# A two-block transformer kernel: modulation sums, probability scaling, post-norm rows and skip columns moved to other places

## The chip, the cores and the metric

The kernel runs on one core of a Trainium2 chip. The metric is device time in microseconds, the median of three runs. The core has a matrix engine (TensorE, PE in the profile, with its weight loads as PEld), VectorE (DVE), ScalarE (ACT), GpSimd (POOL) and a DMA-issuing engine (SyncE, SP). Each engine works through its own line of instructions in order and waits on semaphores where it needs another engine's result or a transfer.

## The reference, cut to what matters

512 tokens of width 1024 pass through a first block and a second block of two layers. In all of them a conditioning vector c gives shifts, scales and gates through a 1024 x 6144 matrix per block or layer (the modulation).

```python
# first block
mod = silu(c) @ w_ada + b_ada                       # six vectors of 1024
h = rms_norm(x, norm_mix) * (1 + sc_m) + sh_m
y = fox_mixer(h, ...)                               # 16 heads of 64, causal, logits + F[t] - F[s]
x = x + g_m * y
h = rms_norm(x, norm_mlp) * (1 + sc_f) + sh_f
x = x + g_f * (square(relu(h @ w_mlp_in)) @ w_mlp_out)
# second block, layer 0: state space (ssd) + latent attention; layer 1: gated linear attention + sparse attention
for layer in range(2):
    shift_m, scale_m, gate_m, shift_f, scale_f, gate_f = silu(c) @ w + b
    h = rmsnorm(x, pre_m) * (1 + scale_m) + shift_m
    x = x + gate_m * rmsnorm(mixers[layer](h), post_m)      # post row = gate * post gain
    h = rmsnorm(x, pre_f) * (1 + scale_f) + shift_f
    x = x + gate_f * rmsnorm((silu(h @ w_gate) * (h @ w_up)) @ w_down, post_f)
# in the ssd mixer: y = ssd(...) + d_skip[:, None] * xs     # one skip factor per head of 64
```

All of it is in float32. The kernel splits each float32 operand into a high and a low part (hi, lo) and does three products (hi hi, hi lo, lo hi).

## The kernel before, in words

The class `Kernel` builds the program stage by stage; a planner of the language (the tile framework) puts each engine's instructions in an order, from their order in the program (a priority), dependencies and its own costs, and gives each tile a buffer of a pool. `self.order(later, earlier)` fixes an order by hand. `behind(n)` lowers the priority of what is inside by n.

*Weights* (`unit`, L130 to 165): each 512 KB piece is loaded on SP (L140), cast to hi on ScalarE (L151), and its lo part subtracted on DVE (L152). `mm3` issues the three products (L120 to L122).

*Start* (`first_modulation`, `first_norm`): x is loaded, then for c = 0, 1 (halves of the width) and part 1, 0 (scale, shift) a piece of the modulation: eight blocks k of 128 rows of w_ada, each multiplied by a column of silu(c) and added up, on DVE (L915, L917) or, for the k in `PADA`, by PE into PSUM (L912). PE then sums the DVE accumulator over partitions with ones (L919); DVE adds the bias (L922) and, for the scale, makes gs. `first_norm` squares x (L385), normalises it (L942), and transposes it with PE (L947) into tiles that ScalarE copies (L949), in two halves, one after each piece of c = 0. `scaled(c)` makes h_hi (L892) and, through a scaled copy that overwrites xt (L894 on ScalarE for odd k, L896 on DVE for even k), h_lo (L897).

*Attention of the first block* (`fox`): eight pairs of heads. `fox_prep` projects q, k, v of a pair; `rsqrt_many` makes the roots on DVE (L750 to L758) and L667 scales q and k by them; `fox_pair` transposes (L733) and splits them, and copies the key's high part to the other half of the partitions on GpSimd (L742). `fox_attend` does four query blocks per head, of 128, 256, 384 and 512 keys: logits on PE (L686 to L688), bias and minimum on DVE (L470), exponential on ScalarE (L99), reciprocal on DVE (L480), scaling of the probabilities (L488 on ScalarE or L490 on DVE by `share`, which is 0 here), transposes (L500) and products with v (L537 to L540). A `Feed` mixes the next pair's preparation into these steps and runs the background modulation (`bg`, `modulation_piece`) for three more of the six vectors. With `ada_tile` set, as here, DVE does its first product (L263), ScalarE the other seven in place (L265), and GpSimd adds them (L266).

*Modulation later on*: in the MLP and FFN stages `bg` accumulates on DVE (L263, L268). With `ada_lag` set, `modulation_pair` folds the accumulator's halves of partitions on GpSimd (a copy L287 and an addition L288) and PE sums two pieces at once (L294).

*State space mixer* (`ssd`, phase mixB2): an own small tile d_col is loaded by two GpSimd transfers (L1255), DVE makes eight diagonal matrices of it (L1258), and PE adds the skip with them (L1354).

*Output projections* (`down_blocks`): per pair of token blocks, per half c of the width and per block, PE makes 128 x 512; `evict` (here `add_to`) adds it to y (L1457) and squares the sum (L385). After c = 1, `post` makes the root of the block (`token_rsqrt`, L391 to L398), then per half u = y * root * row (L1379), x += u (L1380) and, if another norm follows, the squares of x. `normalized` (L436) and `modulate` (transposes L417, scalings L421 to L428) make the next h from it. At the very end `store_x` (L461) writes x.

## Time and profile before

| what | value |
|---|---|
| median of 3 runs | 2299.11 us (2297.29 to 2301.78) |
| the profiled execution | 2299.34 us, its span 2297.5 us |
| mean granted TensorE clock | 0.98 |
| PE, DVE, ACT, POOL busy | 96%, 64%, 47%, 12% of the span |
| moved by DMA | 274.82 MB, mean 120 GB/s |
| chain that ended last | PE 71%, DVE 14%, ACT 6%, DMA 5%, issue 3% |

The profile shows one execution. A row of a group gives line, engine, operation, output <- inputs and shape, a count, busy us and the mean ns of one, and then the idle time ahead of it with its releaser. A row of waits gives the waiting engine and line, what released it, the total us, the number of waits and the longest. A row of the timeline gives start, length, the instruction, and in brackets the idle time ahead of it. A row of the DMA issues gives destination <- source, queue, count, KB of one, and us from issue to landing (a median). PE's busy time is modelled from pipelined matmuls.

### The profile page before, as it was taken

The page shows a single profiled execution, that of the slowest core. Times are in us where ns is not written, and L with a number is a line of the kernel's source. Part 1 is how long each engine was busy: PE and PEld are TensorE (multiplying, and loading weights), DVE is VectorE, ACT ScalarE, POOL GpSimd, SP SyncE. Part 2 cuts the span into 40 slices and gives each one's busy share as a digit, 9 for nine tenths or more (in the row PEclk, how much of TensorE's full clock was granted, in tenths as well). Part 3 has the DMA queues.
Part 4 walks back from the last instruction along what each step waited for, and adds up shares of the span by engine and source line. Part 5 has one row for each costly group of instructions (what it writes and reads, how often), then busy time and mean ns, then how long its engine had stood idle before and what let it go on. Part 6 is the DMA issues. An engine that isn't in the chain of part 4 may idle for free.

```text
span 2297.5 us, 31560 instructions
## 1 busy us (share of the span) xinstructions
PE 2196.5 (96%) x11520; PEld 1845.2 (80%) x11520; DVE 1473.4 (64%) x3232; ACT 1081.9 (47%) x2132; POOL 266.8 (12%) x298
## 2 busy tenths in 40 slices
PE   6899999999999999899999999999999999999998
PEld 6778778788878777778988888877888878888886
DVE  5888877665537898586655563754899557322425
ACT  5677655333234656456432132644777346332322
POOL 0333200110000100210001010101434000000000
PEclk8999999999999999999999999999999999999999
DMA  7544245654533222214556463243111343331412
GB/s 228 149 147 147 65 133 179 229 198 147 176 121 117 75 66 65 37 41 153 165 177 199 160 206 101 85 121 109 31 49 32 98 142 92 110 110 56 138 47 82
DMA packets 210523, 274.82 MB, mean 120 GB/s; under 512 B 19488, under 2 KB 134896, under 8 KB 209600
## 3 DMA queue, kind: packets, MB, share of 16 engines
q1 hardware_dynamic: 205424, 254.03, 35.5%
q0 software_dynamic: 3648, 14.44, 2.3%
q10 hardware_dynamic: 1296, 4.34, 0.5%
q8 instruction: 91, 1.49, 0.3%
q14 instruction: 64, 0.52, 0.1%
HBM read 264.31 MB, written 8.45 MB: 119 GB/s over the span
## 4 chain that ended last, share of the span: by engine, by line
PE 71%; DVE 14%; ACT 6%; DMA 5%; issue 3%; SPq 0%; POOL 0%; DVEq 0%; ACTq 0%; POOLq 0%
PE mm L120 21%; PE mm L122 21%; PE mm L121 21%; DVE wlo L152 1%; ACT whi L151 1%; DVE p L490 1%; DMA ada<-w_ada 1%; DVE pt L116 1%; PE tp L500 1%; DVE p L470 1%; DMA hid<-w_ada 1%; PE o L1618 1%; PE tot L417 1%; PE yd L1310 1%; DMA d_col<-l_d_skip 1%
## 5 line engine op out<-in xcount | busy, mean ns | idle before, releaser
L120 PE MATMUL mm<-h_hi,whi 128*128 128x512 f32 (+1 forms) x920 | 330.9, 360 | 0.8 <-ACT hid L1014 0.4
L121 PE MATMUL mm<-h_lo,whi 128*128 128x512 f32 (+1 forms) x920 | 329.4, 358 | 0.1
L122 PE MATMUL mm<-h_hi,wlo 128*128 128x512 f32 (+1 forms) x920 | 329.1, 358 | 0.4 <-DVE wlo L152 0.4
L152 DVE TENSOR_TENSOR wlo<-wraw,whi 128x1024 fp32r<-128x1024 f32 (+3 forms) x194 | 235.9, 1220 | 135.9 <-ACT whi L151 134.7
L151 ACT CAST whi<-wraw 128x1024 fp32r<-128x1024 f32 (+3 forms) x194 | 199.5, 1032 | 195.5 <-PE mm L121 88.0
L120 PE MATMUL mm<-whi,h_hi 128*128 128x256 f32 (+3 forms) x544 | 192.0, 356 | 7.0 <-ACT whi L151 4.5
L120 PEld LDWEIGHTS mm<-h_hi,whi 128*128 128x128 f32 x920 | 173.9, 189 | 28.9 <-issue 0.8
L122 PEld LDWEIGHTS mm<-h_hi,wlo 128*128 128x128 f32 x920 | 173.9, 189 | 27.1 <-DVE wlo L152 0.9
L121 PEld LDWEIGHTS mm<-h_lo,whi 128*128 128x128 f32 x920 | 174.0, 189 | 25.4 <-DVE h_lo L428 0.4
L151 ACT CAST whix<-wraw 128x1024 fp32r<-128x1024 f32 x104 | 108.4, 1054 | 177.0 <-PE mm L122 85.5
L121 PE MATMUL mm<-wlo,h_hi 128*128 128x256 f32 (+3 forms) x544 | 186.2, 344 | 0.7 <-DVE wlo L152 0.7
L122 PE MATMUL mm<-whi,h_lo 128*128 128x256 f32 (+3 forms) x544 | 185.2, 342 | 0.0
L120 PE MATMUL mm<-h_hi,whix 128*128 128x512 f32 (+1 forms) x496 | 183.7, 370 | 1.5 <-ACT whix L151 1.5
L268 DVE SCALAR_TENSOR_TENSOR ada_acc<-ada,cols,ada_acc 128x512 f32<-128x512 f32 x182 | 137.4, 755 | 73.1 <-DMA ada<-l_ada_w 65.1
L121 PE MATMUL mm<-h_lo,whix 128*128 128x512 f32 (+1 forms) x496 | 183.3, 370 | 0.0
L122 PE MATMUL mm<-h_hi,wlox 128*128 128x512 f32 (+1 forms) x496 | 183.2, 369 | 0.0
L152 DVE TENSOR_TENSOR wlox<-wraw,whix 128x1024 fp32r<-128x1024 f32 x104 | 130.7, 1262 | 66.3 <-ACT whix L151 65.4
L120 PE MATMUL mm<-whi,hid 128*128 128x512 f32 x416 | 168.9, 407 | 1.8 <-ACT whi L151 1.7
L121 PE MATMUL mm<-wlo,hid 128*128 128x512 f32 x416 | 166.3, 400 | 1.2 <-DVE wlo L152 1.1
L122 PE MATMUL mm<-whi,hid 128*128 128x512 f32 x416 | 165.1, 399 | 2.2 <-DVE hid L116 2.2
L121 PE MATMUL mm<-wlox,hid 128*128 128x512 f32 x320 | 125.8, 393 | 0.0
L122 PE MATMUL mm<-whix,hid 128*128 128x512 f32 x320 | 125.8, 393 | 0.0
(488 smaller groups left out, 4773.8 us busy)
## 6 DMA issues: line engine op xcount, KB each, us to landing
ada<-l_ada_w SPq DMA_DIRECT2D x192, 256.0 KB, 4.4
wraw<-l_w_in SPq DMA_DIRECT2D x54, 512.0 KB, 3.8
wraw<-l_w_gate SPq DMA_DIRECT2D x44, 512.0 KB, 4.8
wraw<-l_w_up SPq DMA_DIRECT2D x44, 512.0 KB, 4.1
wraw<-l_w_down SPq DMA_DIRECT2D x44, 512.0 KB, 3.7
wraw<-w_mlp_in SPq DMA_DIRECT2D x32, 512.0 KB, 4.4
wraw<-w_mlp_out SPq DMA_DIRECT2D x32, 512.0 KB, 4.8
hid<-w_ada SPq DMA_DIRECT2D x48, 256.0 KB, 5.0
```

Of the source, the lines that this page charges most:

```text
L116: self.nc.vector.tensor_sub(lo, x, hi.bitcast(F32))
L120: mm(ps, a[0], b[0], start=start, stop=False)
L121: mm(ps, a[0], b[1], start=False, stop=False)
L122: mm(ps, a[1], b[0], start=False, stop=stop)
L151: nc.scalar.copy(hi[:, :nk, :n], raw[:, :nk, :n])
L152: nc.vector.tensor_sub(lo[:, :nk, :n], raw[:, :nk, :n], hi[:, :nk, :n].bitcast(F32))
L268: nc.vector.scalar_tensor_tensor(acc, raw, c, acc, op0=OP.mult, op1=OP.add)
L417: nc.tensor.transpose(ps[:, e, b * 128:b * 128 + 128], xns[b][k // 4][:, c:c + 128], self.ident)
L470: nc.vector.tensor_tensor_reduce(out=p[:, :n], in0=S[:, :n], in1=bias, scale=-1.0, scalar=3e38, op0=OP.add, op1=OP.min, accum_out=st[:, 0:1])
L490: nc.vector.tensor_scalar(p[:, :n], p[:, :n], st[:, 2:3], None, op0=OP.mult)
L500: nc.tensor.transpose(tp[:w, j * 128:(j + 1) * 128], p[:, j * 128:j * 128 + w], self.ident)
L1310: nc.tensor.matmul(yd[:, c:c + 64], m[:, j], xd[g][:, c:c + 64], start=False, stop=q + j == 4)
```

## The change

The modulation beside the attention now uses the DVE form with one instruction per product and sum, and the fold uses ScalarE for the copy and DVE for the addition. `share` is 3 in the attention of the first block: of each four softmaxes, the second to fourth (256, 384 and 512 keys) are scaled on ScalarE. The key copy of pair 0 is done by ScalarE from PSUM. In the start, k = 5 goes from PE to DVE; both pieces of a half are accumulated before PE sums either and before the biases are added; the first half of the norm stands between these, and the second half behind the last of these sums; `scaled` writes its copy to a tile of its own, on ScalarE for all k of the first half. In `down_blocks` the eviction already multiplies y by the post row, so that `post` is one instruction per half; in the last FFN the last 128 x 512 is done in two halves of 256 columns. The skip factors become eight columns of the table that is loaded at the start. (The square's scratch tile is cut to the operand's width for this.)

```diff
@@ -61,7 +61,7 @@
-PADA = (3, 5, 7)
+PADA = (3, 7)
@@ -261,9 +261,6 @@
                 nc.vector.tensor_scalar(acc, raw, c, None, op0=OP.mult)
-            elif self.ada_tile:
-                nc.scalar.activation(raw, raw, AF.Copy, scale=c)
-                nc.gpsimd.tensor_add(acc, acc, raw)
@@ -284,8 +281,8 @@
         s = self.t("fs")
-        nc.gpsimd.tensor_copy(s[mine], acc[other])
-        nc.gpsimd.tensor_add(self.fold[mine], acc[mine], s[mine])
+        nc.scalar.copy(s[mine], acc[other])
+        nc.vector.tensor_add(self.fold[mine], acc[mine], s[mine])
@@ -381,7 +378,7 @@
-        junk = self.t("sq")
+        junk = self.t("sq")[:, :v.shape[-1]]
@@ -554,7 +551,7 @@
         ready, vs = {}, [[] for _ in range(4)]
-        self.share, self.tlag = 0, 1
+        self.share, self.tlag = 3, 1
@@ -667,7 +664,7 @@
         def pair():
-            out[p] = self.fox_pair(qk, self.kl[p % 2])
+            out[p] = self.fox_pair(qk, self.kl[p % 2], p == 0)
@@ -723,7 +720,7 @@
-    def fox_pair(self, qk, kl):
+    def fox_pair(self, qk, kl, first):
@@ -739,7 +736,10 @@
                 nc.vector.scalar_tensor_tensor(lo, ps[r], g[r], dst[r, e].bitcast(F32), op0=OP.mult, op1=OP.subtract)
-            nc.gpsimd.tensor_copy(kh[x, e], kh[r, e].bitcast(F32))
+            if first:
+                nc.scalar.activation(kh[x, e], pst[1][r], AF.Identity, scale=self.col["fox_k"][r])
+            else:
+                nc.gpsimd.tensor_copy(kh[x, e], kh[r, e].bitcast(F32))
@@ -787,7 +787,7 @@
-        def evict(b, c, ps, st):
+        def evict(b, c, ps, st, q):
@@ -802,7 +802,7 @@
-        def evict(b, c, ps, st):
+        def evict(b, c, ps, st, q):
@@ -890,13 +890,15 @@
                 nc.scalar.activation(hi, xt[k], AF.Identity, scale=g, bias=sh)
-                if k % 2:
-                    nc.scalar.activation(xt[k], xt[k], AF.Identity, scale=g, bias=sh)
+                u = self.t("u")
+                if k % 2 or c == 0:
+                    nc.scalar.activation(u, xt[k], AF.Identity, scale=g, bias=sh)
                 else:
-                    nc.vector.tensor_scalar(xt[k], xt[k], g, sh, op0=OP.mult, op1=OP.add)
-                nc.vector.tensor_sub(lo, xt[k], hi.bitcast(F32))
+                    nc.vector.tensor_scalar(u, xt[k], g, sh, op0=OP.mult, op1=OP.add)
+                nc.vector.tensor_sub(lo, u, hi.bitcast(F32))
...
         for c in range(2):
+            pieces = []
@@ -912,20 +914,27 @@
                     elif k == 0:
-                        nc.vector.tensor_scalar(acc, raw[:, 0], s, None, op0=OP.mult)
+                        last = nc.vector.tensor_scalar(acc, raw[:, 0], s, None, op0=OP.mult)
                     else:
-                        nc.vector.scalar_tensor_tensor(acc, raw[:, k % 2], s, acc, op0=OP.mult, op1=OP.add)
+                        last = nc.vector.scalar_tensor_tensor(acc, raw[:, k % 2], s, acc, op0=OP.mult, op1=OP.add)
+                pieces.append((i, acc, ps))
+            if c == 0:
+                next(norm)
+            for i, acc, ps in pieces:
                 for j in range(4):
-                    nc.tensor.matmul(ps[:, j:j + 1], acc[:, j * 128:(j + 1) * 128], self.ones[:, 0:1],
-                                     start=False, stop=j == 3)
-                q = slice(c * 4, c * 4 + 4)
-                nc.vector.tensor_add(mod[:, i * 4:i * 4 + 4], ps[:, :4], self.col["bA"][:, i * 4:i * 4 + 4])
-                if part:
-                    nc.vector.scalar_tensor_tensor(gs[:, q], mod[:, i * 4:i * 4 + 4], 1.0, self.col["gA"][:, q],
-                                                   op0=OP.add, op1=OP.mult)
-                    nc.vector.tensor_scalar(gs[:, q], gs[:, q], NORM, None, op0=OP.mult)
-                if c == 0:
-                    next(norm, None)
+                    mm = nc.tensor.matmul(ps[:, j:j + 1], acc[:, j * 128:(j + 1) * 128], self.ones[:, 0:1],
+                                          start=False, stop=j == 3)
+            q = slice(c * 4, c * 4 + 4)
+            for i, acc, ps in pieces:
+                add = nc.vector.tensor_add(mod[:, i * 4:i * 4 + 4], ps[:, :4], self.col["bA"][:, i * 4:i * 4 + 4])
+                self.order(add, last)
+            nc.vector.scalar_tensor_tensor(gs[:, q], mod[:, 8 + c * 4:12 + c * 4], 1.0, self.col["gA"][:, q],
+                                           op0=OP.add, op1=OP.mult)
+            nc.vector.tensor_scalar(gs[:, q], gs[:, q], NORM, None, op0=OP.mult)
+            if c == 0:
+                self.after = mm
+                next(norm)
@@ -944,7 +953,9 @@
                 for b in range(4):
-                    nc.tensor.transpose(ps[:, b * 128:b * 128 + 128], x[b][:, k * 128:k * 128 + 128], self.ident)
+                    i = nc.tensor.transpose(ps[:, b * 128:b * 128 + 128], x[b][:, k * 128:k * 128 + 128], self.ident)
+                    if c:
+                        self.order(i, self.after)
@@ -1249,10 +1260,7 @@
-        dcol = self.tmp.tile([128, 8], F32, name="d_col")
-        for i in range(2):
-            src = self.a["l0_d_skip_2"].rearrange("(o c i) -> i o c", i=2, o=1)[i]
-            nc.gpsimd.dma_start(dcol[i * 64:i * 64 + 64], src.to_broadcast([64, 8]))
+        dcol = self.col["d_skip"]
@@ -1369,15 +1377,14 @@
-    def post(self, x, y, row, b, st, sums=True):
+    def post(self, x, us, b, st, sums=True):
...
             f = slice(c * 512, c * 512 + 512)
-            u = self.t("u")
-            nc.vector.scalar_tensor_tensor(u, y[:, b, f], r, row[:, f], op0=OP.mult, op1=OP.mult)
-            nc.vector.tensor_add(x[:, b, f], x[:, b, f], u)
+            nc.vector.scalar_tensor_tensor(x[:, b, f], us[c], r, x[:, b, f], op0=OP.mult, op1=OP.add)
@@ -1397,21 +1404,23 @@
-    def down_blocks(self, w, k0, xs, evict, after, gain=None, done=0, first=None):
+    def down_blocks(self, w, k0, xs, evict, after, gain=None, done=0, first=None, split=False):
...
         for pair in range(2):
-            st = [self.stats() for _ in range(2)]
+            st, us = [self.stats() for _ in range(2)], [[], []]
...
                     ps = self.mm.tile([128, T], F32, name="mm")
-                    self.tm(ps, ws[c], 0, 512, xs[skip[c]:], b)
-                    evict(b, c, ps, st[e])
+                    for q in ((0, 256), (256, 512)) if split and b == 3 and c else ((0, 512),):
+                        self.tm(ps[:, q[0]:q[1]], ws[c], *q, xs[skip[c]:], b)
+                        us[e] += evict(b, c, ps, st[e], q) or []
                     if c and first:
-                        st[e] = first(b, st[e])
+                        st[e] = first(b, st[e], us[e])
@@ -1451,14 +1460,26 @@
-    def add_to(self, y):
-        def evict(b, c, ps, st):
-            v = y[:, b, c * 512:c * 512 + 512]
-            self.nc.vector.tensor_add(v, v, ps)
-            self.squares(st, c, v)
+    def add_to(self, y, row):
+        def evict(b, c, ps, st, q):
+            if q[0] == 0:
+                self.uy = self.t("uy")
+            f = slice(c * 512 + q[0], c * 512 + q[1])
+            v, u = y[:, b, f], self.uy[:, q[0]:q[1]]
+            self.nc.vector.tensor_add(v, v, ps[:, q[0]:q[1]])
+            if q == (0, 256):
+                self.squares(st, 4, v)
+            elif q == (256, 512):
+                self.squares(st, 1, v)
+                self.nc.vector.tensor_add(st[:, 1:2], st[:, 1:2], st[:, 4:5])
+            else:
+                self.squares(st, c, v)
+            self.nc.vector.tensor_mul(u, v, row[:, f])
+            return [self.uy] if q[1] == 512 else []
...
-    def ffn(self, h, wg, wu, wd, y, first, after):
+    def ffn(self, h, wg, wu, wd, y, row, first, after, last):
@@ -1477,7 +1498,7 @@
                 self.finish()
-                self.down_blocks(wd, p0 * 2, hid, self.add_to(y), after, first=first)
+                self.down_blocks(wd, p0 * 2, hid, self.add_to(y, row), after, first=first, split=last)
@@ -1517,14 +1538,14 @@
                 self.modulate(self.xn, m["gf"], m["sf"], b // 2, LAG[2][b // 2])
-        self.down_blocks(w, 0, cat, self.add_to(y), mid, self.col["ssm_g" if l == 0 else "gla_g"],
-                         first=lambda b, st: self.post(x, y, pm, b, st))
+        self.down_blocks(w, 0, cat, self.add_to(y, pm), mid, self.col["ssm_g" if l == 0 else "gla_g"],
+                         first=lambda b, st, us: self.post(x, us, b, st))
...
         go = self.into(x, l + 1, LAG[3])
-        self.ffn(self.h, *[a[f"l{l}_{n}_2"] for n in ("w_gate", "w_up", "w_down")], y,
-                 lambda b, st: self.post(x, y, pf, b, st, self.has(l + 1)), go)
+        self.ffn(self.h, *[a[f"l{l}_{n}_2"] for n in ("w_gate", "w_up", "w_down")], y, pf,
+                 lambda b, st, us: self.post(x, us, b, st, self.has(l + 1)), go, not self.has(l + 1))
@@ -2038,7 +2059,7 @@
     COLUMNS += [(f"b{_l}", 48)] + [(f"{n}{_l}", 8) for n in ("pre_m", "post_m", "pre_f", "post_f")]
-COLUMNS += [("conv_w", 48), ("conv_b", 12), ("qa_g", 3), ("kva_g", 2), ("ssm_g", 8), ("gla_g", 8), ("b_gk", 4), ("pos", 16)]
+COLUMNS += [("conv_w", 48), ("conv_b", 12), ("qa_g", 3), ("kva_g", 2), ("ssm_g", 8), ("gla_g", 8), ("b_gk", 4), ("pos", 16), ("d_skip", 8)]
@@ -2048,14 +2069,15 @@
              ssm_g=a["l0_ssm_norm_g_2"], gla_g=np.concatenate([a["l1_gla_norm_g_2"].ravel()] * 4),
-             b_gk=a["l1_b_gk_2"], pos=a["l1_cmp_pos_2"])
+             b_gk=a["l1_b_gk_2"], pos=a["l1_cmp_pos_2"],
+             d_skip=np.repeat(a["l0_d_skip_2"].ravel(), 64))
...
     out["columns"] = np.ascontiguousarray(np.concatenate([np.reshape(v[k], (r, 128)) for k, r in COLUMNS]).T)
-    del out["x"]
+    del out["x"], out["l0_d_skip_2"]
```

2 lines of the change are left out of this document (1 added, 1 removed).

## The prediction

> **What bounds the kernel.** I read the page's busy times first.
>
> ```profile
> span 2297.5 us, 31560 instructions
> ...
> PE 2196.5 (96%) x11520; PEld 1845.2 (80%) x11520; DVE 1473.4 (64%) x3232; ACT 1081.9 (47%) x2132; POOL 266.8 (12%) x298
> ```
>
> TensorE (PE) is busy for 96%, and the change takes next to no matmul away. It can therefore win only from the 2297.5 - 2196.5 = 101 us in which PE stands still, and from the time in which its clock is halved. So the second view is PE's own waits:
>
> ```profile
> PE yd L1354 <- DVE diag L1258: 7.1, 1, 7.1
> PE tp L500 <- DVE p L490: 6.4, 11, 1.9
> PE mm L733 <- DVE qk L667: 6.1, 3, 4.6
> PE tot L417 <- ACT xn L436: 4.0, 6, 1.5
> PE tot L294 <- POOL hid L288: 2.2, 1, 2.2
> ```
>
> Each of these five ends on something that the diff touches. The third view, busy times by stretch, puts them in place. Columns: stretch, its length, busy us of PE, PEld, DVE, ACT, POOL, then the granted clock, the DMA share and GB/s.
>
> ```profile
> 0.00:60.00 60.00, 41.92 (x225) 40.17 (x226) 32.42 (x87) 31.38 (x56) 2.19 (x8) 0.86 0.71 226
> 60.00:88.00 28.00, 23.41 (x128) 22.40 (x127) 24.19 (x44) 18.31 (x45) 13.04 (x12) 0.94 0.67 203
> 88.00:302.00 214.00, 197.02 (x1260) 166.59 (x1258) 189.29 (x549) 154.35 (x357) 62.94 (x65) 1.00 0.36 109
> 400.00:415.00 15.00, 10.93 (x35) 8.24 (x34) 10.65 (x16) 5.54 (x9) 1.86 (x2) 0.66 0.80 268
> 928.00:941.00 13.00, 5.95 (x24) 5.09 (x23) 4.98 (x14) 2.48 (x6) 0.00 (x0) 0.74 0.66 137
> 1475.00:1487.00 12.00, 9.01 (x47) 7.88 (x46) 6.45 (x18) 8.71 (x19) 5.22 (x15) 0.72 0.24 81
> ```
>
> PE stands still for 18.1 us in the start, 4.6 in the preparation of the attention, 17.0 in the attention, 4.1, 7.0 and 3.0 in the three short stretches. A clock of 0.74 over 13 us is half speed for about 6.8 us: after a gap the matmuls also run slow, and a gap that goes takes that with it.
>
> **A. Skip columns (-8.5 us).** The eight diag multiplications wait for two tiny transfers of d_col:
>
> ```profile
> wraw<-l_w_in SPq DMA_DIRECT2D x1, 512.0 KB, 12.7
> ...
> 935.34 1.66 DVE L1258 TENSOR_SCALAR diag<-ident,d_col 128x128 f32<-128x128 f32 x8 [6.83 <-DMA d_col<-l_d_skip]
> 935.68 2.08 PE L1354 MATMUL yd<-diag,hid 128*128 128x128 f32 x8 [7.05 <-DVE diag L1258]
> 936.57 1.05 ACT L151 CAST whix<-wraw 128x1024 fp32r<-128x1024 f32 x1 [11.48 <-DMA wraw<-l_w_in]
> ...
> 937.62 0.78 PE L120 MATMUL mm<-whix,h_hi 128*128 128x512 f32 x1
> ```
>
> ```profile
> wraw<-l_w_in SPq DMA_DIRECT2D x54, 512.0 KB, 3.8
> ```
>
> The first row is the one weight transfer of that stretch: 12.7 us to landing, where the 54 of its kind take 3.8. It is issued at 936.57 - 12.7 = 923.9 and stands in the same DMA engines as d_col, so it is the next thing that could be late. With the column in the table at the start both go: the weights land near 923.9 + 3.8 = 927.7, their cast ends 1.05 later at 928.8. PE, free at 935.68 - 7.05 = 928.6, does the eight diag matmuls at full clock (2.08 / 2 = 1.0 us) and is at the weights by about 929.9 instead of 937.62: 7.7 us. Of the 6.8 us at half speed at most 941 - 937.62 = 3.4 lie behind that row, worth at most 1.7; I add 1.3: 9.0. I take 8.5 because diag's eight instructions (1.66 us) must now find a place on VectorE (DVE) among the weight residuals. Ends: 6 if they delay one residual by their whole length, 9.5 if nothing is lost. Eight more columns (4 KB) in a load of the start are under a hundredth of one 512 KB weight transfer; I put them at nothing.
>
> The Trainium skill, "TensorE: Matmul & The Clock Gate", Part 1, says that the clock is halved after about one idle window of 3.4 us; the gap of 7.05 us with its half clock agrees. By its advice under Why this matters for your kernels, to allow no gap over about 3 us, the stretch 400 to 415, whose single gaps are 2.2 us at most, should have stayed at full speed, and its row says 0.66: the row decides, and short gaps in a row count too.
>
> **B. First modulation (-5.5 us).** Before, each piece's sum is closed by PE (L919) before the next piece's accumulation stands in DVE's line:
>
> ```profile
> DVE mod_modA L922 <- PE psA L919: 15.4, 4, 6.2
> ```
>
> ```profile
> 18.24 0.75 DVE L917 SCALAR_TENSOR_TENSOR ada_acc<-ada,cols,ada_acc 128x512 f32<-128x512 f32 x1
> 20.65 1.71 PE L919 MATMUL psA<-onesr,ada_acc 128*128 128x1 f32 x8
> 31.35 1.52 ACT L892 ACTIVATE h_hi<-hid,mod_modA,gsA 128x512 fp32r<-128x512 f32 x2 [3.09 <-DVE mod_modA L922]
> 47.45 0.16 DVE L922 TENSOR_TENSOR mod_modA<-psA,cols 128x4 f32<-128x4 f32 x1 [6.23 <-PE psA L919]
> 47.92 0.48 DVE L915 TENSOR_SCALAR ada_acc<-ada,cols 128x512 f32<-128x512 f32 x1
> 54.51 1.70 PE L120 MATMUL mm<-whi,h_hi 128*128 128x400 f32 x4 [1.85 <-ACT whi L151]
> ```
>
> After: the first piece ends at 18.24 + 0.75, plus one more accumulation because k = 5 leaves PE (0.75): 19.7. The second piece follows at once: 0.48 + 5 x 0.75 = 4.2, so 23.9. PE's closing sums take 1.7 (if the first piece's are done ahead) to 3.4, four small DVE instructions about 0.7: 26.3 to 28.0 instead of 31.35, 3.3 to 5.0 us. In the second half the 6.23 us in which DVE waits for PE goes too; its price is again one more accumulation, 0.75. That adds up to about 9 us where the half resumes (54.51). Against it stand: the second four transposes' ScalarE copies now fall beside the scaling, all four u of the first half move to ScalarE, and PE's matmuls of the first half must themselves be through. I take 5.5, between the ends 1 and 8.
>
> **C. Preparation of the attention (-4.5 us).** GpSimd (POOL) adds the modulation's products here. While one runs, DVE instructions of a fraction of a microsecond take far longer; the chain's ends, and between them the same line twice:
>
> ```profile
> 73.41 1.19 DVE L753 TENSOR_SCALAR r<-r 128x16 int32<-128x16 int32 x1
> ...
> 76.03 0.17 DVE L758 SCALAR_TENSOR_TENSOR r<-rs_t,r 128x16 f32<-128x16 f32 x1
> ...
> 80.75 2.11 DVE L758 SCALAR_TENSOR_TENSOR r<-rs_t,r 128x16 f32<-128x16 f32 x1
> 82.90 1.43 DVE L667 TENSOR_TENSOR qk<-qk,r 128x256 f32<-128x256 f32 x4
> ```
>
> The chain of roots to qk (L667), for which PE waits 4.6 us in one piece, runs from 73.4 to 82.9; some twelve such instructions at 0.17 would be 2.1, so some 7 us is contention. Six accumulations at 0.75 = 4.5 us come to DVE in their place. If all six stand in the chain it is 2.8 us shorter; if none, 7 shorter, of which PE can use its 4.6 and the 1.7 that the clock (0.94 over 28 us) costs. I take 4.5; ends 1.5 and 6.3.
>
> The Trainium skill, "SBUF — State Buffer", Who interferes with whom, has GpSimd and VectorE share a port pair under an exclusive lock; the two rows fit that. "Perfetto Trace Analysis", Optimizing Scalar/DVE Operations, would rather take work off a full DVE, which speaks against this edit; by it the loss would be the 31.7 us of the next part, with no 15 us won back.
>
> **D. The attention itself (-1.5 us).** What moves, from the groups between 60 and 310 us:
>
> ```profile
> L490 DVE TENSOR_SCALAR p<-p,st 128x512 f32<-128x512 f32 x16 | 10.6, 663 | 0.2
> L490 DVE TENSOR_SCALAR p<-p,st 128x256 f32<-128x256 f32 x16 | 8.6, 535 | 0.1
> L490 DVE TENSOR_SCALAR p<-p,st 128x384 f32<-128x384 f32 x16 | 8.3, 521 | 0.2
> L265 ACT ACTIVATE hid<-hid,cols 128x512 f32<-128x512 f32 x42 | 28.8, 719 | 3.6 <-DMA hid<-w_ada 3.5
> L266 POOL TENSOR_TENSOR hid<-hid 128x512 f32<-128x512 f32 x42 | 56.9, 1355 | 114.1 <-ACT hid L265 87.7 <-ACT pt L113 24.4
> ```
>
> ```profile
> L268 DVE SCALAR_TENSOR_TENSOR ada_acc<-ada,cols,ada_acc 128x512 f32<-128x512 f32 x182 | 137.4, 755 | 73.1 <-DMA ada<-l_ada_w 65.1
> ```
>
> With share = 3 the three wider blocks of each head go to ScalarE, the 128-wide one stays. DVE gains 42 x 0.755 = 31.7 us and loses 10.6 + 8.6 + 8.3 = 27.5. The contention goes as well: a 128x512 TENSOR_SCALAR took 0.48 alone (L915 above) and 0.663 here, 0.28 of it lost. POOL is busy for 62.94 of the 214 us; if DVE loses that share while it is, 189.3 x 62.94 / 214 x 0.28 is an estimate of 15 us. Net about -11 of 189. ScalarE loses 28.8 and gains at most 48 x 0.719 = 34.5: even. So neither engine gets heavier, and PE's 17.0 us of waiting could shrink. But the scaling now takes a second engine between the reciprocal and the transpose (0.72 for 0.48 at full width), the exponentials behind it wait for that reciprocal, and DVE now stands still when a modulation transfer is late. I take -1.5; ends +6 and -8. The key copy of pair 0 on ScalarE is two instructions and goes with this.
>
> **E. Post rows ahead of the root (-2 us at 1475, -1.3 at the end).** The count is equal, but one of the two instructions per half moves ahead of the root, into the time of ScalarE's square. The last block:
>
> ```profile
> 2291.88 1.41 DVE L1379 SCALAR_TENSOR_TENSOR u<-yacc,stats,row 128x512 f32<-128x512 f32 x2
> 2293.21 1.29 DVE L1380 TENSOR_TENSOR x<-x,u 128x512 f32<-128x512 f32 x2
> ```
>
> The 1.29 goes. The split last eviction halves the add and the square ahead of the root, and pays with one more small DVE add and twice as many, half as wide matmuls; I put it at nothing, between a loss of 0.9 and a gain of 0.3 (estimates). So 1.3, ends 0.4 and 1.6. Before 1475 two blocks follow one another, so 2 x 1.3 less a row product of 0.7 that now stands ahead of the root: 2. The gap there is 3.0 us with a clock of 0.72, so up to 5; 0 if the next weights are late instead. The products stay in the phase's eight scratch buffers until the root; a pair's fourth takes the buffer that the post of the block before frees, which stands ahead of it in DVE's line anyway: nothing, but there E could become a wait.
>
> **F. Folds (-0.5 us).** 26 pairs leave POOL; one pair is waited for, in 400 to 415:
>
> ```profile
> 405.50 0.60 POOL L287 COPY fs<-ada_acc 64x512 f32<-64x512 f32 x1 [11.12 <-DVE ada_acc L268]
> 406.18 1.26 POOL L288 TENSOR_TENSOR hid<-ada_acc,fs 64x512 f32<-64x512 f32 x1
> ```
>
> 1.94 us becomes at most 0.72 + 0.75. The other 25 pairs put under 20 us each on ScalarE and DVE, over stages in which PE is the bound and both have room. What is queued behind the ScalarE copy (casts, evictions) now waits for DVE's last accumulation. Ends: -3.5 (clock loss goes) and +3.
>
> **Sum.** 8.5 + 5.5 + 4.5 + 1.5 + 2 + 1.3 + 0.5 = 23.8 off 2297.5: span 2273.7. The profiled execution took 2299.34, 1.8 outside the span: **2275.5 us**, 23.6 under the median 2299.11 of runs from 2297.29 to 2301.78; a shift within 0.2% (4.6 us) can't be told from none.
>
> **Rivals.**
> 1. *The attention stops on its transfers* (slower). In the later layers L268 waits 65.1 us for DMA in 182 instructions, 0.36 each; 42 of them would be 15 us on a DVE that has 214 - 189.3 = 25 us to spare. With 0.2 us more for each of 48 scalings (9.6), and nothing hidden, D is +25 instead of -1.5: 2275.5 + 26.5 = 2302. It decides once D costs over 22.3 us, the rest's gain. Against it: L265 waited only 3.6 us for the same transfers. 6%.
> 2. *The start is set by its transfers*, and the new order wins nothing (B = 0): 2281. For it, the chain of waits of the first 100 us names DMA ada first; against it, DVE's waits there are on PE (15.4), not on DMA. 18%.
> 3. *Another stall takes d_col's place*, the weights at 936.57 being late for other reasons (A = 1.5): 2282.5. Against it, 3.8 for all others. 8%.
> 4. *The attention was bound by the contention*: D = -8, B = -8: 2266.5. For it, PE's 6.4 us behind L490. 14%.
> 5. The planner places things otherwise and most terms come at their poor ends (1.5 + 6 + 1 + 0.4 - 4): 2294. 8%.
>
> The forecast itself has 46%. **Range** 2263 to 2290: it leaves out the poorest cases and the tip of 4. Faster 0.91 (all but 1 and half of 5), same 0.04, slower 0.05.
>
> **What would show it.** A: no wait of yd on diag, and full clock near 930. B: h_hi first at 27 to 29 and matmuls of the second half by 50. C: the wait of L733 under 1.5 us, no L758 over 0.3. D: PE busy over 198 of a like stretch, and no new wait of tp on ACT p over 6 us. E: the gap before 1480 under 1.5 us. Wrong: DVE waiting on hid<-w_ada by over 10 us, or the start at 54 as before.

## The result, and the profile after

The changed kernel takes **2260.2 us** (median of 2258.90 to 2268.39) against 2300.39 us for the kernel before beside it: a ratio of 0.9829, 95% interval 0.9802 to 0.9855. Timed a second time it was 2264.09 against 2299.29 us: 0.9843, interval 0.9817 to 0.9868. So 35 to 40 us are gained, where 23.6 were forecast: the sign is right, and the time lies below the foot of the range (2263) the first time and just inside it the second.

The profiled execution is the longest of the first set: 2268.39 us with a span of 2266.4, 31.1 us less than the span before. Its page and TensorE's waits, in the order of those shown of before:

```profile
span 2266.4 us, 31372 instructions
...
PE 2185.7 (96%) x11512; PEld 1837.8 (81%) x11512; DVE 1462.2 (65%) x3257; ACT 1100.8 (49%) x2170; POOL 143.6 (6%) x200
```

```profile
PE tot L414 <- ACT xn L433: 2.8, 4, 1.0
PE tp L497 <- ACT p L485: 2.4, 5, 0.5
...
PE mm L730 <- DVE qk L664: 2.2, 1, 2.2
...
PE tot L291 <- DVE hid L285: 1.7, 1, 1.7
```

TensorE stands still for 2266.4 - 2185.7 = 80.7 us instead of 101.0, and it is busy for 10.8 us less with nearly the same matmuls, which fits the granted clock (0.980 before, 0.986 here). The 7.1 us of yd on diag are gone, and tp's 6.4 us on VectorE's scaling have become 2.4 us on ScalarE's and 0.9 on VectorE's. The stretches that answer to those of before (same columns; the later ones start earlier by what was won until there):

```profile
60.00:88.00 28.00, 23.94 (x140) 22.81 (x139) 25.41 (x60) 16.86 (x41) 1.59 (x3) 1.00 0.64 195
82.00:284.00 202.00, 195.35 (x1266) 167.77 (x1265) 179.46 (x538) 159.74 (x371) 16.83 (x30) 1.00 0.38 115
382.00:397.00 15.00, 12.23 (x43) 9.38 (x42) 12.30 (x19) 4.30 (x8) 0.00 (x0) 0.77 0.82 275
903.00:916.00 13.00, 12.82 (x65) 9.65 (x65) 10.82 (x20) 6.97 (x12) 1.71 (x2) 1.00 0.37 122
1450.00:1462.00 12.00, 10.42 (x84) 9.80 (x84) 8.15 (x21) 10.61 (x22) 3.65 (x4) 1.00 0.14 32
```

The second row is the point of this case: the attention, 214 us before, is 202 long, and TensorE's idle time in it fell from 17.0 to 6.7 us.

**Where the time went, by marks.** The weight matmuls of line 120 are the same in every run, so the start of the n-th one can be compared. A mark carries the time that it has in the kernel before: mark 78 is the 55th (77.7 us), 113 the 85th, 350 the 321st, 891 the 1121st, 957 the 1161st, 1467 the 1881st, 1491 the 1921st, 1955 the 2441st. The table shows how many us later (+) or earlier (-) one profiled execution of each kernel reaches them than the profile of before. Runs are named by what the sections below change.

| run | 78 | 113 | 350 | 891 | 957 | 1467 | 1491 | 1955 | end |
|---|---|---|---|---|---|---|---|---|---|
| changed kernel, first | -2.0 | -5.5 | -18.8 | -18.2 | -25.0 | -24.7 | -29.4 | -30.5 | -31.1 |
| changed kernel, again | -2.9 | -4.8 | -17.0 | -16.2 | -23.0 | -22.7 | -27.4 | -33.7 | -34.3 |
| same, old start | +2.9 | -1.9 | -16.1 | -15.0 | -24.8 | -24.7 | -29.3 | -35.1 | -35.7 |
| same, folds on GpSimd, no split | -3.7 | -7.1 | -20.7 | -20.2 | -27.0 | -26.3 | -31.4 | -33.9 | -35.5 |
| before + A, B, E | -4.4 | -0.5 | +3.4 | +3.1 | -3.6 | -1.3 | -6.3 | -7.7 | -8.2 |
| before + scalings | +2.9 | +2.8 | -4.2 | -3.1 | -0.4 | -0.3 | -0.2 | -4.1 | -4.1 |
| before + products | +1.9 | -4.6 | +4.9 | +5.2 | +8.1 | +8.2 | +6.9 | +0.1 | +0.1 |
| before + both | +1.4 | -5.2 | -19.9 | -18.8 | -16.0 | -15.3 | -15.3 | -21.4 | -21.4 |
| before - GpSimd's additions | +3.0 | -3.9 | -14.0 | -14.4 | -14.4 | -14.4 | -14.4 | -18.5 | -18.5 |

Two cautions come out of it. Kernels with the same old start differ by up to 3 us at mark 78, and kernels whose code between 1491 and 1955 is that of before (the last four rows) win 4 to 7 us there against its profile: that profile was late in this part. Most of it is the clock: between these two marks the same matmuls keep TensorE busy for 441.4 us before and for 435.0 to 439.2 in those four (440.8 and 435.2 in the changed kernel's two). A difference of 2 or 3 us in one row is therefore no finding.

### The profile page after: what moved, and what is told of

Its sections match the earlier page's. It is cut to its first block, busy times and chain, and to the rows that moved or that the text cites. A ratio compares the mean times of both kernels' runs of the same rounds, so it can differ in the third digit from the quotient of the medians.

```text
span 2266.4 us, 31372 instructions
## 1 busy us (share of the span) xinstructions
PE 2185.7 (96%) x11512; PEld 1837.8 (81%) x11512; DVE 1462.2 (65%) x3257; ACT 1100.8 (49%) x2170; POOL 143.6 (6%) x200
## 4 chain that ended last, share of the span: by engine, by line
PE 77%; DVE 11%; ACT 5%; DMA 5%; issue 2%; SPq 0%; ACTq 0%; DVEq 0%
PE mm L120 22%; PE mm L122 22%; PE mm L121 22%; PE tp L497 1%; DVE wlo L152 1%; ACT whi L151 1%; DMA ada<-w_ada 1%; DVE pt L116 1%; DMA ada<-l_ada_w 1%; PE tot L414 1%; DVE p L487 1%; PE o L1639 1%; PE o L535 1%; PE yd L1318 1%; ACT sq L382 1%
## 5 line engine op out<-in xcount | busy, mean ns | idle before, releaser
L121 PE MATMUL mm<-h_lo,whix 128*128 128x512 f32 (+1 forms) x496 | 183.3, 370 | 0.0
L120 PE MATMUL mm<-whix,hid 128*128 128x512 f32 (+1 forms) x328 | 127.6, 389 | 0.6 <-DVE yacc L1470 0.6
L121 PE MATMUL mm<-wlox,hid 128*128 128x512 f32 (+1 forms) x328 | 127.4, 388 | 0.0
```

The source lines that it names most:

```text
L120: mm(ps, a[0], b[0], start=start, stop=False)
L121: mm(ps, a[0], b[1], start=False, stop=False)
```

## Experiments: the two moves of the attention

Theory 1: VectorE's total work paces the attention. Theory 2: only the contention with GpSimd did. Theory 3, the forecast's: the scaling's second engine costs about what is won.

**Scalings alone.**

```
-        self.share, self.tlag = 0, 1
+        self.share, self.tlag = 3, 1      # in fox()
```

> The kernel before, with the probability scalings of the attention alone moved: 3 of 4 on ScalarE (share = 3). The modulation stays on ScalarE and GpSimd. Theory 1 (the attention is paced by VectorE's total work): VectorE loses 27.5 of 189 us and the stage from 88 to 302 shortens by 15 to 25 us, unless ScalarE (154 + 34 of 214 us) takes its place. Theory 2 (only the contention with GpSimd paced it): GpSimd works as before, so the stage moves by less than 4 us. Theory 3 (the scaling's second engine on the way from root to transpose costs, as the forecast of part D had it): the stage is longer by 0 to 10 us.

Measured: 2293.47 us, ratio 0.9972 (0.9960 to 0.9985).

**Products alone.**

```
-            elif self.ada_tile:
-                nc.scalar.activation(raw, raw, AF.Copy, scale=c)
-                nc.gpsimd.tensor_add(acc, acc, raw)
             else:
                 nc.vector.scalar_tensor_tensor(acc, raw, c, acc, op0=OP.mult, op1=OP.add)
```

> The kernel before, with the products of the modulation beside the attention alone moved to VectorE (one multiply-add each, 42 of 0.755 us), no share on ScalarE changed, folds on GpSimd as before. Theory 1 (VectorE's total work): VectorE gains 31.7 us and loses about 15 of contention, so the stage from 88 to 302 is 10 to 17 us longer. Theory 2 (contention alone): the stage is 8 to 14 us shorter. Both: the preparation from 60 to 88 is about 3 us shorter.

Measured: 2301.42 us, ratio 1.0007 (0.9997 to 1.0017).

**Both.**

> The kernel before with both moves, 3 of 4 scalings on ScalarE and the modulation's products on VectorE. If these two edits hold the whole gain between 60 and 302 us of the changed kernel (3.1 + 13.3), the program is 14 to 18 us shorter than before. Theory 1 wants this to lie near the sum of the two single moves; theory 2 wants it near the second move alone.

Measured: 2279.32 us, ratio 0.9916 (0.9901 to 0.9931), 20 us less than the kernel before beside it and more than the 14 to 18 expected.

The stretch from mark 113 to mark 350 in each (columns as above: stretch, length, busy us of PE, PEld, DVE, ACT, POOL, clock, DMA share, GB/s). Expectations that speak of 226.7 or 233 us count from a mark 3.6 us earlier. The kernel before:

```profile
113.38:349.64 236.26, 217.41 (x1319) 181.64 (x1318) 197.53 (x543) 164.11 (x365) 58.28 (x61) 0.98 0.39 123
```

The changed kernel:

```profile
107.86:330.80 222.94, 214.05 (x1319) 181.01 (x1318) 188.09 (x532) 167.00 (x374) 16.43 (x29) 0.98 0.40 127
```

Scalings alone, products alone, both:

```profile
116.19:345.46 229.27, 215.19 (x1319) 181.42 (x1318) 177.81 (x500) 183.24 (x406) 58.54 (x61) 0.98 0.39 124
```

```profile
108.83:354.58 245.75, 223.62 (x1318) 189.13 (x1318) 203.53 (x575) 145.47 (x333) 16.57 (x29) 0.94 0.37 118
```

```profile
108.19:329.78 221.59, 214.57 (x1319) 181.37 (x1318) 187.93 (x532) 166.99 (x375) 16.44 (x29) 0.98 0.40 128
```

The scalings alone bring 236.3 - 229.3 = 7.0 us, the products alone cost 9.5, both together bring 14.7: they don't add, and no theory has all three. Theory 2 falls with the second run: GpSimd's additions are gone (16.57 us are left), and the stretch is longer, with 203.5 us of VectorE. Theory 3 falls with the first and third. Theory 1 has the signs of the single moves, but missed the first by more than half and would have had the third near their sum. The preparation (marks 78 to 113) does go by theory 2: it gains 0.1 us with the scalings alone, some 6.5 in both runs with the products off GpSimd.

**GpSimd's work put back.**

```
                 nc.vector.scalar_tensor_tensor(acc, raw, c, acc, op0=OP.mult, op1=OP.add)
+                if self.ada_tile:
+                    nc.gpsimd.tensor_add(raw, raw, raw)
```

> The changed kernel with 42 additions on GpSimd put back beside the attention (each product's 128x512 tile added to itself after VectorE has read it; the result is not used), so GpSimd is busy for about 57 us again and VectorE's own instructions are the same. If contention is worth 0.28 of the time that GpSimd is busy: VectorE's busy time in the attention rises by 15 us, and the stage is longer by 8 to 15 us (theories 1 and 2 alike). If contention is worth nothing, less than 2 us.

Measured: 2290.49 us, ratio 0.9955 (0.9932 to 0.9978): most of the change's gain is gone. Its stretch, and three groups between 55 and 310 us (line, engine, operation, shapes, count; busy us, mean ns; idle before):

```profile
114.19:359.02 244.83, 225.87 (x1318) 189.36 (x1317) 205.02 (x532) 166.78 (x375) 55.51 (x61) 0.94 0.37 116
```

```profile
L267 POOL TENSOR_TENSOR hid<-hid 128x512 f32<-128x512 f32 x42 | 50.9, 1224 | 128.1 <-DVE hid L265 96.3 <-DMA hid<-w_ada 19.4 <-issue 7.9
L265 DVE SCALAR_TENSOR_TENSOR hid<-hid,cols 128x512 f32<-128x512 f32 x42 | 47.4, 1133 | 2.5 <-DMA hid<-w_ada 2.3
...
L116 DVE TENSOR_TENSOR pt<-tp,pt 128x512 fp32r<-128x512 f32 x14 | 9.6, 682 | 5.9 <-ACT pt L113 5.7
```

In the changed kernel the same groups are:

```profile
L265 DVE SCALAR_TENSOR_TENSOR hid<-hid,cols 128x512 f32<-128x512 f32 x42 | 31.3, 749 | 2.6 <-DMA hid<-w_ada 2.4
...
L116 DVE TENSOR_TENSOR pt<-tp,pt 128x512 fp32r<-128x512 f32 x16 | 10.9, 681 | 0.3
```

The same 532 VectorE instructions take 16.9 us more, nearly all of it in the multiply-adds (1133 instead of 749 ns), and the stretch is 21.9 us longer where 8 to 15 were expected: the extra busy time was about right (15), its price was not.

## Experiments: a dose for each engine

A dose is extra work for one engine whose result nobody uses; what the kernel then loses is the price of that engine's time.

**Dose on VectorE.** The line `nc.vector.tensor_scalar(raw, raw, c, None, op0=OP.mult)` is added behind each product, under `if self.ada_tile:`.

> The changed kernel with a dose of work for VectorE: 42 multiplications of a 128x512 tile beside the attention (0.48 us each, the result is not used), 32 of them between the marks 110 and 350 of the kernel before, 15 us in all. Theory 1, in the form that the four runs before gave it (the stage moves by 1.3 to 1.45 us for each us of VectorE's busy time): the stretch is 18 to 23 us longer than the changed kernel's. Rival (TensorE, busy for 218 of 227 us, is now the bound, and VectorE has 37 us to spare): under 5 us longer.

**Half of it** (`if self.ada_tile and k % 2:`).

> The changed kernel with about half of the dose for VectorE: 24 multiplications of a 128x512 tile beside the attention (0.48 us each, result not used), 18 of them between the marks, 8.7 us. Between the marks the changed kernel has 188 us of VectorE in 223 us, the full dose 200 in 244. If the loss grows in proportion above a knee at 188: 235 to 238 us. If it comes only when VectorE is over some 195 us: under 228.

**Dose on ScalarE** (`nc.scalar.activation(raw, raw, AF.Copy, scale=c)` in the same place).

> The changed kernel with a dose of work for ScalarE: 42 scaled copies of a 128x512 tile beside the attention (0.72 us each, result not used), 32 of them between the marks, 23 us, so ScalarE is busy for about 192 us as in the run with only the scalings moved (186). If VectorE alone paces the attention: under 3 us longer. If the fuller of the two engines does: 5 to 10 us longer, as that run had 233 us for the stretch where the changed kernel has 226.7.

**All scalings on ScalarE** (share = 4).

> The changed kernel with all four of four probability scalings on ScalarE (share = 4): VectorE loses 16 x 0.31 = 5 us, ScalarE gains 16 x 0.4 = 6.4 us. Theory 1: the attention is 4 to 7 us shorter and the program 0.2 to 0.3% faster than the changed kernel. If TensorE is now the bound, or ScalarE (169 + 6 us) is as near: within 2 us of it.

The same stretch, in this order:

```profile
107.55:351.85 244.30, 226.15 (x1319) 189.56 (x1318) 200.19 (x564) 167.83 (x375) 16.39 (x29) 0.94 0.36 116
```

```profile
107.68:336.98 229.30, 215.86 (x1318) 181.33 (x1317) 194.40 (x550) 167.79 (x374) 16.34 (x29) 0.98 0.39 124
```

```profile
105.97:330.98 225.01, 215.92 (x1318) 181.23 (x1317) 188.81 (x532) 184.28 (x406) 16.50 (x29) 0.98 0.40 126
```

```profile
106.12:332.86 226.74, 214.13 (x1318) 180.30 (x1317) 186.77 (x518) 171.73 (x390) 16.50 (x29) 0.98 0.41 128
```

The full dose adds 12.1 us to VectorE and 21.4 us to the stretch, although VectorE has some 35 us without work in it: the rival, that TensorE alone is now the bound, falls. Half of it adds 6.3 to VectorE and 6.4 to the stretch, below the 12 to 15 that a straight line from 188 had asked for and a little above the other expectation (229.3 for under 228). ScalarE takes 17.3 us more at a cost of 2.1. With share = 4 the 14 narrow scalings of the stretch leave VectorE (4.3 us by their own lengths, though its busy time falls by only 1.3), and the stretch is 3.8 us longer than in the changed kernel's first profile, where theory 1 asked for 4 to 7 shorter. Five profiles of kernels with both moves lie between 221.6 and 224.0 us, so 226.7 is outside their scatter. Timed, that kernel has 2267.77 us, ratio 0.9867 (0.9842 to 0.9891): no better than the changed one, which neither expectation had.

**GpSimd's additions left out of the kernel before**, with the scalings where they were, and with the scalings moved:

```
                 nc.scalar.activation(raw, raw, AF.Copy, scale=c)
-                nc.gpsimd.tensor_add(acc, acc, raw)
```

> The kernel before without GpSimd's 42 additions beside the attention, nothing else changed: the modulation's sums beyond their first product are left out, the products on ScalarE stay, and VectorE still does every scaling. Asked is what the contention alone was worth. Between marks 113 and 350 the kernel before takes 236.3 us with 197.5 us of VectorE. Estimate from the rows of both kernels: VectorE is busy for about 183 us. If VectorE's busy time alone decides, with a knee near 188 us: 222 to 225 us. If the contention costs by the moments at which it strikes, as the run without the additions but with the scalings moved (4.0 us) suggests: 230 to 233 us.

> The kernel before with 3 of 4 scalings on ScalarE, as in the run with only the scalings moved, and without GpSimd's 42 additions: the modulation's sums beyond their first product are left out, the products on ScalarE stay. ScalarE has as much to do as in that run (186 us), GpSimd nothing. If contention with GpSimd kept that run at 233 us between marks 112 and 350: 226 us or less, as with both moves. If ScalarE's products in the middle of its line did: 231 to 234 us.

The stretch in the first and in the second, then one group of the first between 55 and 310 us:

```profile
109.49:335.62 226.13, 216.61 (x1318) 181.30 (x1317) 183.26 (x543) 163.73 (x365) 16.51 (x29) 0.98 0.41 129
```

```profile
109.31:334.56 225.25, 215.28 (x1318) 182.20 (x1317) 171.32 (x500) 183.54 (x407) 16.50 (x29) 0.97 0.40 126
```

```profile
L489 DVE TENSOR_SCALAR p<-p,st 128x512 f32<-128x512 f32 x16 | 7.7, 483 | 0.2
```

The same 543 VectorE instructions as before take 183.3 instead of 197.5 us: the contention was **14.3 us** (the scaling of 128x512 alone fell from 663 to 483 ns). It was worth 10.1 us in the stretch and, at the marks 78 to 113, 6.9 us in the preparation. (No wait of the kernel before is put down to one of the additions there, so it hardly is their results that came sooner.) With the scalings moved as well VectorE has 12 us less still, and the stretch gains 0.9. The run with the scalings alone had missed 4.0 us of its 229.3 by contention; the rest above the changed kernel's 222.9, 2.3 us, is about what ScalarE's dose costs. The first of these runs came near its first expectation (222 to 225), the second, with about 229 us counted as there, between its two.

The mean of 663 ns hides what contention is. In the kernel before, 14 of the 16 scalings of 128x512 take 0.47 to 0.49 us, and two take 1.93. Here is one of the two, a GpSimd addition that runs beside it, and one of the 14:

```profile
175.93 1.93 DVE L490 TENSOR_SCALAR p<-p,st 128x512 f32<-128x512 f32 x1
176.28 2.72 POOL L266 TENSOR_TENSOR hid<-hid 128x512 f32<-128x512 f32 x2
251.27 0.49 DVE L490 TENSOR_SCALAR p<-p,st 128x512 f32<-128x512 f32 x1
```

In this group few instructions are hit, and each is then longer by about one whole addition (2.72 us for two): a stop, and no rate.

Put in order of VectorE's busy time:

| kernel | VectorE, us | stretch, us | TensorE busy | TensorE idle |
|---|---|---|---|---|
| before - additions, + scalings | 171.3 | 225.2 | 215.3 | 10.0 |
| before + scalings | 177.8 | 229.3 | 215.2 | 14.1 |
| before - additions | 183.3 | 226.1 | 216.6 | 9.5 |
| changed, share = 4 | 186.8 | 226.7 | 214.1 | 12.6 |
| before + both | 187.9 | 221.6 | 214.6 | 7.0 |
| changed | 188.1 | 222.9 | 214.1 | 8.9 |
| changed + ScalarE's dose | 188.8 | 225.0 | 215.9 | 9.1 |
| changed + half dose | 194.4 | 229.3 | 215.9 | 13.4 |
| before | 197.5 | 236.3 | 217.4 | 18.8 |
| before + A, B, E | 200.2 | 240.2 | 220.0 | 20.2 |
| changed + dose | 200.2 | 244.3 | 226.2 | 18.2 |
| before + products | 203.5 | 245.7 | 223.6 | 22.1 |
| changed + GpSimd's additions | 205.0 | 244.8 | 225.9 | 19.0 |

There is a **floor** at 222 to 227 us, where TensorE is busy for 214 to 217 and less work on VectorE brings nothing more. Above some 190 us of VectorE a slope follows that begins near 1 and reaches 2 to 3 between 194 and 200, where the clock joins in (granted 0.94 instead of 0.98 in the last three rows, 10 to 12 us more of busy TensorE for the same matmuls); above 200 the three differ by no more than 1.4 us. The scalings alone lie above the floor, with GpSimd's additions still there. The slope is rough: the same attention code takes 236.3 us before and 240.2 before + A, B, E (clock 0.98 and 0.96). The kernel before stood on the slope, the changed one stands at its foot. Slices of 20 us show why VectorE's time without work is no slack; the kernel before, then the changed one at nearly the same work:

```profile
128.00:148.00 20.00, 18.00 (x149) 17.08 (x148) 17.95 (x54) 15.70 (x35) 8.73 (x9) 1.00 0.58 184
148.00:168.00 20.00, 18.87 (x108) 14.91 (x106) 18.89 (x58) 14.19 (x33) 5.26 (x6) 1.00 0.57 177
```

```profile
124.00:144.00 20.00, 19.48 (x154) 18.00 (x152) 19.56 (x54) 16.25 (x37) 1.76 (x3) 1.00 0.59 192
144.00:164.00 20.00, 19.98 (x113) 16.18 (x112) 19.51 (x66) 14.62 (x38) 1.76 (x3) 1.00 0.48 156
```

Before, both engines stand at 18 to 18.9 of 20 us in the same slice, and neither is full. After, both are above 19.4 in these slices. And VectorE's free time before is itself waiting, for ScalarE above all: of 24.3 us without work from 108 to 302 us, ScalarE ends 17.6 (the longest waits: total, times, longest):

```profile
DVE st L480 <- ACT p L99: 5.8, 10, 0.9
DVE wlo L152 <- ACT whi L151: 4.8, 6, 0.9
DVE pt L116 <- ACT pt L113: 4.7, 10, 0.9
```

So the work passes round: TensorE waits for VectorE, VectorE for ScalarE. That added work makes the next link late, and does not fall into these waits, is my reading of the dose; no single wait shows it.

## Experiments: the other parts

**A, B and E alone** (the kernel before with the new start, the skip columns and the post rows with the split).

> The kernel before with parts A (skip columns), B (start) and E (post rows, split last eviction) alone; the attention, its preparation and the folds stay as before. The parts lie far apart in time, so each is read by itself. If the parts stand for themselves: 6 to 7 us near 930, 4 to 5 near 1475 and about 1 after it, 2.4 in the start, nothing between 110 and 350; 13 to 15 us in all. If A or E won something only because the attention ended earlier, less than this.

Measured: 2288.72 us, ratio 0.9951 (0.9937 to 0.9965), 9.7 us less than the kernel before beside it, where 13 to 15 were expected. A brings 6.7 and E 5.0 us here as in the changed kernel, so both stand for themselves. The start's 4.4 us are down to 0.5 at mark 113: TensorE waits 8.4 us in one piece for qk there, against 4.6 before. At mark 350 the kernel is 3.4 late, with the attention's code unchanged and a lower clock in it (0.96 for 0.98).

**The old start in the changed kernel** (first_modulation and first_norm as before, PADA = (3, 5, 7)), and the changed kernel itself beside it:

> The changed kernel with the old start (first modulation and first norm in the old order, three products of a piece on TensorE); all else as changed. If the new start keeps what it wins (6 us against the old starts of these runs): the program is about 6 us, 0.25%, slower than the changed kernel. If the preparation of the attention gives most of it back, as in the run with parts A, B and E alone (4.4 ahead at mark 78, 0.5 at mark 113): within 3 us of it at mark 113.

> The changed kernel itself, a second time. Its first profile had the matmuls at mark 78 only 2.0 us ahead of the kernel before, while four other kernels with the same new start had them 3.8 to 4.4 ahead, and three with the old start were 1.4 to 2.9 behind. If the start scatters from execution to execution by some 2 us, this profile is like those: 3.8 to 4.4 ahead at mark 78 and a span of 2258 to 2264. The attention (marks 113 to 350) again 11 to 14 us shorter than before. If the first profile is the rule: 2.0 ahead again and 2266.

Measured: 2264.40 us (2263.79 to 2267.88) with the old start, 2264.09 (2261.60 to 2265.49) with the new. No difference can be told. At mark 78 the new start is 5.8 us ahead of the old one, at mark 113 still 2.9, as the second expectation had it, at 350 still 0.9, and at 957 nothing (-23.0 against -24.8; the clock ahead of part A, below, differs there). The second profile of the changed kernel did not come out as far ahead as expected, but in between: the start scatters.

**Folds on GpSimd, and no split of the last eviction.**

```
-        nc.scalar.copy(s[mine], acc[other])
-        nc.vector.tensor_add(self.fold[mine], acc[mine], s[mine])
+        nc.gpsimd.tensor_copy(s[mine], acc[other])
+        nc.gpsimd.tensor_add(self.fold[mine], acc[mine], s[mine])
...
-                 lambda b, st, us: self.post(x, us, b, st, self.has(l + 1)), go, not self.has(l + 1))
+                 lambda b, st, us: self.post(x, us, b, st, self.has(l + 1)), go, False)
```

> The changed kernel with its folds on GpSimd again (part F undone) and without the split of the last eviction; the first is read between marks 350 and 1470, the second behind mark 2270. Part F as forecast: 0.5 us longer between 400 and 420, between 3.5 longer and 3 shorter in all. The split: nothing, between 0.3 longer without it and 0.9 shorter.

Measured: 2264.40 us, ratio 0.9846 (0.9822 to 0.9871). From mark 350 to mark 891 it loses 0.5 us, the changed kernel 0.6 and 0.8: F is nothing. At the end it gains 1.6 us behind mark 1955, where the changed kernel gains 0.6, so the split **costs 1.0**. The last eviction in the changed kernel, then without the split:

```profile
2255.52 0.41 DVE L1470 TENSOR_TENSOR yacc<-yacc,mm 128x256 f32<-128x256 f32 x1
2255.99 0.39 PE L120 MATMUL mm<-whix,hid 128*128 128x256 f32 x1 [0.64 <-DVE yacc L1470]
...
2259.16 0.42 DVE L1470 TENSOR_TENSOR yacc<-yacc,mm 128x256 f32<-128x256 f32 x1 [1.57 <-PE mm L122]
```

```profile
2254.10 0.39 PE L122 MATMUL mm<-whix,hid 128*128 128x512 f32 x1
2254.53 0.69 DVE L1470 TENSOR_TENSOR yacc<-yacc,mm 128x512 f32<-128x512 f32 x1 [0.90 <-PE mm L122]
```

The second half's matmuls write into the same psum tile and wait until VectorE has read the first half (0.64 us); all 24 of them stand behind that wait.

## Why the prediction was wrong, by its steps

**D is the step that failed.** Its account of busy time holds: VectorE was to lose 11 us net and lost 197.5 - 188.1 = 9.4, ScalarE was to stay even and has 167.0 for 164.1 us. The contention was estimated at 15 us and is 14.3, but that is luck: the share of 0.28 came from the mean of 14 scalings that lost nothing and two that were stopped, and was taken as a rate for all of VectorE's work. What failed is the price of the sentence that neither engine gets heavier "and PE's 17.0 us of waiting could shrink": 1.5, at best 8. Of the 17.0 us, waits that VectorE ended make 14.9 and those that ScalarE ended 1.8; in the like stretch of the changed kernel they are 1.5 and 5.1. With 9.4 us less on VectorE the attention became 12.2 to 14.2 us shorter (marks 113 to 350 in four profiles of kernels with the whole attention changed). I took the 25 us in which VectorE did not work in the stage for slack; the dose shows that they are none. What the second engine in the chain costs was not measured by itself; it is small (the wait of tp on ScalarE's scaling is 2.4 us, and ScalarE's dose of 17.3 us costs 2.1). Rival 4, the contention as the bound, was the nearest, with 14%: contention alone brings 10.1 us in the attention and 6.9 before it; its other term, a start at its best end, has nothing to do with contention. Rival 1 falls: VectorE waits for the modulation's transfers for 2.4 us, not 15.

The Trainium skill's "SBUF — State Buffer", Who interferes with whom, is borne out by the runs without GpSimd's additions and by the 1.93 us of a scaling beside one: it has one engine hold the shared ports for a whole instruction and the other blocked, not slowed. The Trainium skill's "Perfetto Trace Analysis", Optimizing Scalar/DVE Operations, which would take work off a full VectorE, is right about the products by themselves (+9.5 us in the attention); the scalings taken off VectorE pay for them. The prediction's price by that section, without the 15 us of contention, was not the section's own: it also warns that GpSimd and VectorE share a port.

**C** was forecast at 4.5 and is 4.8 to 6.9 us with the old start, 1.3 to 3.5 with the new one. The chain of roots in the changed kernel:

```profile
78.09 0.17 DVE L758 SCALAR_TENSOR_TENSOR r<-rs_t,r 128x16 f32<-128x16 f32 x1
78.51 1.42 DVE L664 TENSOR_TENSOR qk<-qk,r 128x256 f32<-128x256 f32 x4
```

The step that took 2.11 us takes 0.17, as foretold; the wait for qk is 2.2 us, not under 1.5. **B** at its own place is right in size: 5.6 us at mark 78, the mean of nine profiles with the new start (-3.5) against seven with the old one (+2.1, with before as 0), forecast 5.5. In this profile the second half resumes at 52.69, 1.8 us ahead and not by 50; but the profile of before is the earliest of the seven with the old start (57.0 in the mean) and this one the latest of the nine with the new (51.2).

```profile
23.84 3.41 PE L914 MATMUL psA<-cols,ada 128*128 128x1 f32 x16
24.57 0.15 DVE L930 TENSOR_TENSOR mod_modA<-psA,cols 128x4 f32<-128x4 f32 x1
27.12 1.84 PE L926 MATMUL psA<-onesr,ada_acc 128*128 128x1 f32 x8
29.33 0.81 ACT L892 ACTIVATE h_hi<-hid,mod_modA,gsA 128x512 fp32r<-128x512 f32 x1 [4.66 <-DVE gsA L934]
52.69 1.70 PE L120 MATMUL mm<-whi,h_hi 128*128 128x400 f32 x4 [2.69 <-ACT whi L151]
```

VectorE ended its part by 24.57 (forecast 23.9), but TensorE closes the second piece's sum only at 28.96: its own products of that piece (L914, 3.41 us) stand ahead of the sum, and the working left them out. The working came to about 9 us and was cut to 5.5 by judgement, so that the size fits is partly luck. And what B wins does not show at the end. With the new start C is worth less, so the sum of the two was too high; that both change VectorE's line there is a likely reason, not a shown one. Where B's last 3 us go between mark 113 and the end is not settled; they are no more than the scatter.

**A** did what its working said:

```profile
wraw<-l_w_in SPq DMA_DIRECT2D x1, 512.0 KB, 3.7
```

```profile
911.77 0.67 DVE L1266 TENSOR_SCALAR diag<-ident,cols 128x128 f32<-128x128 f32 x3
912.57 1.04 ACT L151 CAST whix<-wraw 128x1024 fp32r<-128x1024 f32 x1 [2.78 <-DMA wraw<-l_w_in]
912.79 1.06 PE L1362 MATMUL yd<-diag,hid 128*128 128x128 f32 x8
```

The weights land in 3.7 us instead of 12.7, the eight diag matmuls take 1.06 us without a wait, and the clock near 910 is 1.00. Between the marks 891 and 957 it looks smaller than the 8.5 forecast, 6.7 to 7.1 us in seven profiles, and larger, 9.6 to 9.8, in three. The first have a halved clock just ahead of the place, which the profile of before did not have. The changed kernel's first profile, the one with the old start, and the kernel before with both moves of the attention (no part A), each at 875 to 890:

```profile
875.00:890.00 15.00, 13.97 (x63) 9.36 (x62) 11.13 (x34) 9.16 (x25) 0.00 (x0) 0.77 0.24 70
```

```profile
875.00:890.00 15.00, 13.83 (x84) 10.07 (x84) 13.80 (x39) 11.42 (x30) 0.00 (x0) 1.00 0.25 70
```

```profile
875.00:890.00 15.00, 13.96 (x66) 9.57 (x65) 10.99 (x34) 8.73 (x24) 0.00 (x0) 0.77 0.21 66
```

The third, with the halved clock and without A, loses 2.8 us between these marks; 2.8 + 6.8 = 9.6, the same as the 9.8 of the second against before, neither of which has it. All sixteen profiles fall in with this: ten have the halved clock there, of which seven with A gain 6.7 to 7.1 us between the marks and three without lose 2.7 to 3.0; of the six that have none, three with A gain 9.6 to 9.8 and three without are level within 0.5. Like against like A is worth 9.6 us, a little over my upper end of 9.5.

**E** near 1475 was sized at 2, ends 0 to 5, and is 4.6 to 5.1: the gap's halved clock goes too (0.72 to 1.00). I had that as the end of the range and should have taken it, as in A. At the tail 1.3 were forecast; the row product ahead of the root brings 1.6 and the split, put at nothing, takes 1.0. **F** is nothing, as forecast within its ends.

By terms at their own places: B and C together 10 forecast, 6 to 9 measured (-6.2 at mark 113 as a mean of seven profiles, against 0 and +2.8 in the two kernels without either); D 1.5 against 12 to 14; A 8.5 against 9.6, of which a halved clock often takes 2.8; E 2 against 5; the tail 1.3 against 0.6. The sum missed by D, and by a little of E.

## What to carry to other kernels

An engine off the critical path that is busy for 88% of a stage is not slack: look at short slices for places where it and the bounding engine are both at nine tenths and neither is full, and price work taken off it there at what the bounding engine stands still, clock included. A group's mean can hide a few long stops among many untouched instructions: look at the single ones before a rate is made of it. Two edits that trade work between engines have to be priced as one: here one alone cost 9.5 us, the other brought 7.0, and both brought 14.7. And a lead won ahead of a stage that another engine paces can be lost in that stage, as the start's was here.

## What the runs showed of the hardware

Contention with GpSimd falls on some forms alone. Multiply-adds of 128x512 went from 749 to 1133 ns and scalings from 483 to 663, while the subtractions that read a psum tile (L116) have 681 and 682 ns with and without it. That is no matter of chance: of the 32 residuals of q and k (L741), which read psum as well, nine run beside an addition of GpSimd in the kernel before, at a mean of 753 ns, and 20 clear of any at 748.

Executions of one kernel differ by the clock: some stretches are halved in one and not in another. The changed kernel's two profiles have spans of 2266.4 and 2263.3 us at mean clocks of 0.986 and 0.988; its shortest executions, with spans of 2256.9 to 2258.5 us, have 0.990 to 0.992. Of the 2297.5 us before, a clock of 0.980 means some 92 us at half speed, of the 2266.4 after some 65: by this estimate up to 13 of the 31 us won are clock. Part of that went with the gaps (0.74 to 1.00 near 910, 0.72 to 1.00 near 1450), part is scatter.
